# GpSimd's two-operand work on the vector engine, later due times in the SSD tails, and products of ones at the start of a hybrid decoder step

## The chip, the cores and the metric

The kernel runs on one core of one Trainium2 chip. The metric is the device time of one execution in microseconds (us); lower is better. The core's engines are called as the profile calls them: PE (TensorE, the matrix products; PEld are its weight loads), DVE (VectorE), ACT (ScalarE), POOL (GpSimd) and SP (SyncE, which here only issues DMAs). Each engine works through its own instructions in order and waits on semaphores for the others.

## The reference

One decoder layer is computed for a prompt of 512 rows and a sample batch of 8 x 4 rows, D = 1024, all in float32. Cut to its skeleton:

```python
def layer_forward(h, lp, ...):
    u = rmsnorm(h, ffn1_pre_g);  h = h + 0.5 * rmsnorm(swiglu(u, wg, wu, wd), ffn1_post_g)
    u = rmsnorm(h, mix_pre_g)
    z, xbc, dt, q, k, v, qi, ki, wi, g_ssd, g_att = split(u @ w_in)
    y_ssd = ssd_branch(z, xbc, dt, ...)        # causal conv, SSD scan in chunks of 128, norm per group
    y_att = sparse attention on the top 256 keys of an indexer
    merged = sigmoid(g_ssd) * (y_ssd @ w_br_ssd) + sigmoid(g_att) * (y_att @ w_br_att)
    h = h + rmsnorm(merged @ w_out, mix_post_g)
    u = rmsnorm(h, mem_pre_g);   h = h + rmsnorm(mem_attend(u, ...) @ w_mo, mem_post_g)
    u = rmsnorm(h, ffn2_pre_g);  h = h + 0.5 * rmsnorm(swiglu(u, ...), ffn2_post_g)

# ssd_branch, per group of 4 heads:
y = y_diag + y_off + d_skip * xs               # y_diag: (C B^T * decay) @ (x * dt)
y = y * silu(z); y = y * rsqrt(mean(y * y over the group's 256 channels) + EPS) * norm_g
```

## The kernel before, in words

**Layout.** Activations are held transposed: 128 channels on the partitions, 544 columns (512 prompt rows and 32 sample rows) in the free direction, in 8 tiles of a channel block each (`k` = 0..7). `hT` is the residual stream, `y` the output of a stage before its norm. Where 256 or 288 columns are worked on at a time, they are the two halves of the 544.

**Products in two parts.** A float32 factor is split into a high part of reduced precision and the rest (`uh`, `ul` for the activations, `wh`, `wl` for the weights), and `mm` (L291) sums three products per channel block: high x high, low x high, high x low (L310). `weights` (L251) loads 512 KB halves on SP, rounds them on ACT (L270, `wh`) and subtracts on DVE (L271, `wl`); the gates' weights are subtracted on POOL instead (`gates`, L1124).

**Order.** Stages are Python generators that emit instructions and yield `(c, d)`: `c` is the PE time that they have just emitted, `d` a delay before they want to go on, both in a planner's microseconds. `weave` (L104) runs the first generator in its list that is due, and so sets the order in which instructions are emitted. The framework then puts each engine's instructions into a fixed order, which follows the emission with exceptions where it takes an operand to be late.

**Start.** `load_x` (L444) loads the first gain, transposes it on PE (L455) and loads x. `first_T` (L459) transposes the first 256 rows of x (L473), with ACT and DVE writing `uh` and `ul`. Then the FFN's products begin.

**Boundaries between stages.** `bound` (L372) applies the post-norm (L385), adds into `hT` (L386, even `k` on DVE, odd `k` on POOL), squares on ACT and sums the squares into `sqh` on POOL, the last on DVE (`sq_acc`, L363: L366, L369, L370), and writes the next stage's `uh`, `ul` (L391, L392). `rms_rows` (L411) sums the squares over channels by a product with ones (`sth`, L419) and takes the root on DVE; `spread` (L430) copies the factor to all partitions (`pgr`, L439).

**SSD.** `ssd` (L1241) weaves three generators: first the indexer's rounds and the sampled attention, second the tails, last the fronts. A front (`ssd_x`, L1295, and `ssd_z`, L1282) makes the convolved x, B, C of a group (tile `XO`, L1326 to L1329) and z; it may run two groups ahead of the tails. A tail (`ssd_y`, L1338) computes C B^T (`pcb`, L1351) and masks it into `cb` (L1353), transposes B (`pbt`, L1357, copied to `Bt`), after a delay of 2.5 transposes x (`pxt`, L1367; `xd`, `xe` on DVE, L1368 and L1370), multiplies the decay `abc` by `cb` (L1380: POOL, except the second half of groups 1 to 4 on DVE), builds the states (`pst`, L1413), handles the sample rows (with DMAs of `Es` on SP and of the new states), multiplies and adds y, and calls `rms` (L333). That sums squares over the group (`st`, L341), takes the root on DVE (L326 to L331), waits a delay of 4.0, and spreads the factor (L352, `psr`, L355); L1522 applies it and y is stored to `yssd_d`. There are 8 groups.

**Merge.** `att_in`, `att_out` (L1723) and then `merge` (L1738) follow. `merge` reads `yssd_d` back into `yt`, splits it (`yh`, `yl`), and for each of 8 tiles `m` multiplies by the gate (L1760, DVE), adds the attention's part (L1761, POOL) and splits the sum, on which `w_out` works next (`project`, L1767).

Of the kernel before, what the change touches and what calls it, by code (L numbers as in the profile page):

```python
# [7 lines left out]
F32 = mybir.dt.float32  # L8
# [5 lines left out]
ALU = mybir.AluOpType  # L14
# [3 lines left out]
P = 128  # L18
T = 544
TP = 512  # L20
# [148 lines left out]
class Net:  # L169
# [42 lines left out]
    def params(self):  # L212
# [29 lines left out]
        nc.scalar.dma_start(self.caus, I["caus"])  # L242
        ex.close()

    def ps1(self, name="ps1"):
        return self.pm.tile([P, 512], F32, tag="pm", name=name)

# [82 lines left out]
            nc.vector.tensor_tensor(t, t, xh, op=ALU.mult)  # L330
            nc.vector.scalar_tensor_tensor(y, t, 1.5, y, op0=ALU.add, op1=ALU.mult)  # L331

    def rms(self, sqs, inv_n, pool):  # L333


        nc = self.nc
        st = self.ps1("st")
        blk = [(i * P, min(P, T - i * P)) for i in range(5)]
        for i, (c0, n) in enumerate(blk):
            for j, sq in enumerate(sqs):  # L340
                nc.tensor.matmul(st[:n, i:i + 1], sq[:, c0:c0 + n], self.ones[:, :1], start=(j == 0), stop=(j == len(sqs) - 1))  # L341
        w = pool.tile([P, 4, 5], F32, tag="nw", name="nw", bufs=2)
        x, xh, y, t = (w[:, i, :] for i in range(4))
        nc.vector.memset(x, 1.0)
        nc.vector.tensor_scalar(x[:, :4], st[:, :4], inv_n, EPS, op0=ALU.mult, op1=ALU.add)
        nc.vector.tensor_scalar(x[:32, 4:], st[:32, 4:5], inv_n, EPS, op0=ALU.mult, op1=ALU.add)
        self.rsqrt(y, x, xh, t)
        yield 0.3, 4.0

        sq = sqs[0]  # L350
        ps = self.ps1("psr")
        nc.vector.tensor_tensor(sq[:, :TP].rearrange("p (i c) -> p i c", i=4), self.ident.unsqueeze(1).broadcast_to([P, 4, P]),  # L352
                                y[:, :4].unsqueeze(2).broadcast_to([P, 4, P]), op=ALU.mult)
        nc.vector.tensor_scalar(sq[:32, TP:], self.ident[:32, :32], y[:32, 4:], None, op0=ALU.mult)
        nc.tensor.matmul(ps, self.ones, sq[:, :TP], start=True, stop=True)  # L355
        nc.tensor.matmul(st[:, 64:96], self.ones[:32, :], sq[:32, TP:], start=True, stop=True)
        yield 1.0
        return ps, st[:, 64:96]
# [13 lines left out]
    def bound(self, half, sq, post_g, pre_g, rt=None):  # L372


        nc, hT, y = self.nc, self.hT, self.y
        r0, n = HALF[half]
        sl = slice(r0, r0 + n)
        if post_g is not None:
            yield 0.0, 3.0
            r = yield from self.rms_h(sq, half)  # L380
        if pre_g is not None:
            acc = self.nw.tile([P, 288], F32, tag="sqh", name="sqh", bufs=2)
        for k in range(8):
            if post_g is not None:
                nc.vector.scalar_tensor_tensor(y[:, k, sl], y[:, k, sl], post_g[:, k:k + 1], r, op0=ALU.mult, op1=ALU.mult)  # L385
                (nc.gpsimd if k % 2 else nc.vector).tensor_tensor(hT[:, k, sl], hT[:, k, sl], y[:, k, sl], op=ALU.add)  # L386
            if pre_g is not None:
                self.sq_acc(acc, hT[:, k, sl], n, k == 0, last=(k == 7))
            if rt is not None:
                g = pre_g[:, k:k + 1]  # L390
                nc.scalar.activation(self.uh[:, k, sl], hT[:, k, sl], AF.Copy, scale=g)  # L391
                nc.vector.scalar_tensor_tensor(self.ul[:, k, sl], hT[:, k, sl], g, self.uh[:, k, sl].bitcast(F32), op0=ALU.mult, op1=ALU.subtract)  # L392
            yield 0.0, 1.0
        if pre_g is None:
            return
        yield 0.0, 4.0 if rt is None else 8.0
        r = yield from self.rms_h(acc, half)
        if rt is not None:
            nc.scalar.copy(rt[:, sl], r)
            return  # L400
        for k in range(8):
            u = self.nw.tile([P, 288], F32, tag="u", name="u", bufs=2)
            nc.vector.scalar_tensor_tensor(u[:, :n], hT[:, k, sl], pre_g[:, k:k + 1], r, op0=ALU.mult, op1=ALU.mult)
            self.split(self.uh[:, k, sl], self.ul[:, k, sl], u[:, :n], nc.gpsimd if k % 4 == 3 else None)
            yield 0.0, 0.9
# [38 lines left out]
    def load_x(self):  # L444


        nc, I = self.nc, self.I
        xs = self.y.rearrange("p k t -> p (k t)")[:, :4 * D].rearrange("p (i k d) -> i p k d", i=4, k=8)
        self.xin = [xs[i] for i in range(4)] + [self.hT[:32, :, HA:HA + P]]
        gr = self.nw.tile([8, P], F32, tag="dg", name="gr", bufs=2)  # L450
        nc.scalar.dma_start(gr, I["ffn1_pre_g"][0].rearrange("(k p) -> k p", p=P))
        for i in range(2):
            nc.sync.dma_start(self.xin[i], I["x_prompt"][0, i * P:(i + 1) * P, :].rearrange("p (k d) -> p k d", k=8))
        ps = self.ps1("ps_g")
        nc.tensor.transpose(ps[:, :8], gr, self.ident[:8, :8])  # L455
        self.g1 = self.cp.tile([P, 8], F32, name="g1")
        nc.vector.tensor_copy(self.g1, ps[:, :8])

    def first_T(self):  # L459


        nc, I = self.nc, self.I
        q = self.row_squares(0, (0,))
        pss = []
        for k in range(8):
            if k == 4:
                self.weights(("ffn1", "g", 0), [I["ffn1_wg"][0][:, :256]], 8)
            if k % 2 == 0:
                ps = self.ps1("pgx")
                pss.append(ps)  # L470
            v = ps[:, k % 2 * 256:(k % 2 + 1) * 256]
            for i in range(2):
                nc.tensor.transpose(v[:, i * P:(i + 1) * P], self.xin[i][:, k, :], self.ident)  # L473
            gk = self.g1[:, k:k + 1]
            nc.scalar.activation(self.uh[:, k, :HA], v, AF.Copy, scale=gk)
            nc.vector.scalar_tensor_tensor(self.ul[:, k, :HA], v, gk, self.uh[:, k, :HA].bitcast(F32), op0=ALU.mult, op1=ALU.subtract)
        self.weights(("ffn1", "u", 0), [I["ffn1_wu"][0][:, :256]], 8)
        for i in range(2, 4):
            nc.sync.dma_start(self.xin[i], I["x_prompt"][0, i * P:(i + 1) * P, :].rearrange("p (k d) -> p k d", k=8))
        nc.sync.dma_start(self.xin[4], I["x_sample"].rearrange("b t (k d) -> (b t) k d", k=8))  # L480
        for c, ps in enumerate(pss):
            (nc.vector.tensor_copy if c % 2 else nc.scalar.copy)(self.hT[:, 2 * c:2 * c + 2, :HA], ps.rearrange("p (k t) -> p k t", k=2))

        def rest():
            self.row_squares(0, (1,), q)
            yield from self.row_factor(q, 0)

        return rest()
# [849 lines left out]
    def ssd_y(self, g, z):  # L1338
        nc, I, O, sp = self.nc, self.I, self.O, self.sp
# [3 lines left out]
        abc = []  # L1343
# [5 lines left out]
        ps = self.ps1("pcb")  # L1349
        for c in range(4):  # L1350
            nc.tensor.matmul(ps[:, c * P:(c + 1) * P], BO[:, c * P:(c + 1) * P], CO[:, c * P:(c + 1) * P], start=True, stop=True)  # L1351
        cb = sp.tile([P, 4, P], F32, tag="cb", name="cb")
        nc.vector.tensor_tensor(cb, ps.rearrange("p (c t) -> p c t", c=4), self.tri.unsqueeze(1).broadcast_to([P, 4, P]), op=ALU.mult)  # L1353
        yield 0.9
        ps = self.ps1("pbt")
# [1 line left out]
            nc.tensor.transpose(ps[:, c * P:(c + 1) * P], BO[:, c * P:(c + 1) * P], self.ident)  # L1357
        Bt = sp.tile([P, 4, P], F32, tag="hT_", name="Bt", bufs=2)
        nc.scalar.copy(Bt.rearrange("p a b -> p (a b)"), ps)
        yield 0.5, 2.5  # L1360
        hcol = lambda t: t.rearrange("p (c h) -> p c h", c=4)[:, :, 4 * g:4 * g + 4]
        xd = sp.tile([P, 4, 4, 64], F32, tag="xd", name="xd")
        xe = sp.tile([P, 4, 4, 64], F32, tag="xe", name="xe")
        for i in range(2):
            ps = self.ps1("pxt")
# [7 lines left out]
        for i in range(2):  # L1373
            for h in range(2):
                for c in range(4):
                    col = c * 32 + 4 * g + 2 * i + h
                    nc.scalar.activation(abc[i][:, h, c * P:(c + 1) * P], abc[i][:, h, c * P:(c + 1) * P], AF.Relu, scale=-1.0,
                                         bias=self.acs[:, col:col + 1])
            nc.scalar.activation(abc[i], abc[i], AF.Exp, scale=-1.0)
            (nc.vector if 1 <= g <= 4 and i else nc.gpsimd).tensor_tensor(abc[i], abc[i], cb.rearrange("p c t -> p (c t)").unsqueeze(1).broadcast_to([P, 2, TP]), op=ALU.mult)  # L1380

        ps = self.ps1("pcs")
        for q in range(3):
# [27 lines left out]
        for c in range(4):  # L1411
            ps = self.ps1("pst")
# [52 lines left out]
        for i in range(2):  # L1465
# [3 lines left out]
            for q in range(2):  # L1469
                ps = self.ps1("pns")  # L1470
# [8 lines left out]
        ps = self.ps1("pfin")  # L1479
# [10 lines left out]
        for i in range(2):  # L1490
# [7 lines left out]
            ps = self.ps1("pY")  # L1498
# [16 lines left out]
        nc.vector.tensor_tensor(zts[0], zts[0], zts[1], op=ALU.add)  # L1515
        sqs = zts[:1]
        yield 0.0, 9.0
        r, rs = yield from self.rms(sqs, 1.0 / 256, sp)
        for i in range(2):
            tl = 2 * g + i  # L1520
            for o, m in ((Y[i][:, :TP], r), (Y[i][:, TP:], rs)):
# [216 lines left out]
    def merge(self, h_d, rest):  # L1738
# [17 lines left out]
        for m in range(8):  # L1756
            w = self.weights(("w_br_ssd", m), [I["w_br_ssd"][0][:, m * P:(m + 1) * P]], 16)
            t = self.gate(0, m, ep)
            ps = result(self.mm(w, ys, 0))
            nc.vector.tensor_tensor(t, ps, t, op=ALU.mult)  # L1760
            nc.gpsimd.tensor_tensor(t, t, y[:, m, :], op=ALU.add)  # L1761
            self.split(self.uh[:, m, :], self.ul[:, m, :], t)
        ex.close()
        self.open_h()
# [320 lines left out]
```

## Time and profile before

| | us |
|---|---|
| median of 3 runs | 2201.06 (2200.52 to 2204.1) |
| the profiled execution | 2201.23 |
| its span, from the first to the last instruction | 2199.4 |
| PE busy in it | 2101.4 (96%) |
| DVE, ACT, POOL busy | 1324.2 (60%), 955.2 (43%), 444.4 (20%) |
| mean granted clock of PE | 0.979 |

A row of a timeline has the start and the duration in us, the engine, the line of the kernel, the operation, out<-in by tile names, the shapes and the count, and in brackets the idle time of the engine before it and what ended it. A row of waits has the total, the number and the longest. A row of windows gives a stretch, its length, the busy time (and number of instructions) of each engine, the mean granted clock of PE, and DMA share and rate. A row of a line or tile gives the durations in ns (least, median, most) and the first and last start in us. PE overlaps its products, so a busy PE isn't PE at its peak, and a product's duration is longer than the distance to the next one.

### The profile page before, as it was taken

The page shows a single profiled execution, that of the slowest core. Times are in us where ns is not written, and L with a number is a line of the kernel's source. Part 1 is how long each engine was busy: PE and PEld are TensorE (multiplying, and loading weights), DVE is VectorE, ACT ScalarE, POOL GpSimd, SP SyncE. Part 2 cuts the span into 40 slices and gives each one's busy share as a digit, 9 for nine tenths or more (in the row PEclk, how much of TensorE's full clock was granted, in tenths as well). Part 3 has the DMA queues.
Part 4 walks back from the last instruction along what each step waited for, and adds up shares of the span by engine and source line. Part 5 has one row for each costly group of instructions (what it writes and reads, how often), then busy time and mean ns, then how long its engine had stood idle before and what let it go on. Part 6 is the DMA issues. An engine that isn't in the chain of part 4 may idle for free.

```text
span 2199.4 us, 41232 instructions
## 1 busy us (share of the span) xinstructions
PE 2101.4 (96%) x16675; PEld 1960.6 (89%) x16675; DVE 1324.2 (60%) x2711; ACT 955.2 (43%) x1821; POOL 444.4 (20%) x461
## 2 busy tenths in 40 slices
PE   7999999999999999998999999999999979999998
PEld 7999999998788678897888889999987879999998
DVE  6543334475697989896677668544563475424455
ACT  6323345345445665453556445323535443222233
POOL 0000011032122302225555641012320320000011
PEclk9999999999999999998999999999999999999999
DMA  6424565347442223355456636564443433233243
GB/s 199 126 82 128 165 203 197 113 133 213 135 127 83 88 77 110 117 157 161 126 174 192 178 106 186 175 190 155 144 149 139 154 115 115 76 96 90 81 131 100
DMA packets 320107, 301.70 MB, mean 137 GB/s; under 512 B 25416, under 2 KB 290632, under 8 KB 318868
## 3 DMA queue, kind: packets, MB, share of 16 engines
q1 hardware_dynamic: 310508, 272.58, 40.5%
q0 software_dynamic: 8448, 25.18, 3.7%
q8 instruction: 131, 2.15, 0.4%
q10 hardware_dynamic: 960, 1.31, 0.2%
q14 instruction: 60, 0.49, 0.1%
HBM read 261.14 MB, written 37.35 MB: 136 GB/s over the span
## 4 chain that ended last, share of the span: by engine, by line
PE 72%; DVE 13%; DMA 6%; ACT 4%; issue 3%; POOL 2%; SPq 0%; DVEq 0%; ACTq 0%; POOLq 0%
PE pg L310 42%; PE pgh L310 14%; PE pmo L591 2%; DVE wl L271 2%; ACT wh L270 2%; DMA wr<-in_ffn_wu 1%; DVE gtm L1077 1%; DVE XO L1326 1%; DMA yt<-yssd_d 1%; DMA abc<-ac_d 1%; PE pmkT L1811 1%; POOL sqh L370 1%; PE pmo L1878 1%; DVE XO L1329 1%; DMA wr<-in_ffn_wg 1%
## 5 line engine op out<-in xcount | busy, mean ns | idle before, releaser
L270 ACT CAST wh<-wr 128x1024 fp32r<-128x1024 f32 (+3 forms) x362 | 341.6, 959 | 512.1 <-PE pg L310 288.2
L271 DVE TENSOR_TENSOR wl<-wr,wh 128x1024 fp32r<-128x1024 f32 (+3 forms) x338 | 391.1, 1171 | 222.6 <-ACT wh L270 215.8
L310 PE MATMUL pg<-uh,wh 128*128 128x256 f32 (+1 forms) x2336 | 504.1, 297 | 0.8 <-DVE zt L1291 0.8
L310 PE MATMUL pg<-ul,wh 128*128 128x256 f32 (+1 forms) x2336 | 493.4, 292 | 0.0
L310 PE MATMUL pg<-uh,wl 128*128 128x256 f32 (+1 forms) x2336 | 491.6, 291 | 0.0
L310 PEld LDWEIGHTS pg<-uh,wh 128*128 128x128 f32 x2336 | 380.4, 191 | 21.2 <-issue 17.2
L310 PEld LDWEIGHTS pg<-ul,wh 128*128 128x128 f32 x2336 | 381.2, 191 | 2.9 <-issue 2.2
L310 PEld LDWEIGHTS pg<-uh,wl 128*128 128x128 f32 x2336 | 380.0, 190 | 1.8 <-issue 1.4
L310 PE MATMUL pgh<-uh,wh 128*128 128x288 f32 (+2 forms) x880 | 260.8, 299 | 9.5 <-ACT wh L270 6.1
L310 PE MATMUL pgh<-uh,wl 128*128 128x256 f32 (+2 forms) x880 | 260.3, 298 | 7.3 <-DVE wl L271 7.3
L310 PE MATMUL pgh<-ul,wh 128*128 128x256 f32 (+1 forms) x880 | 257.1, 294 | 0.0
L310 PEld LDWEIGHTS pgh<-uh,wh 128*128 128x128 f32 (+1 forms) x880 | 170.4, 195 | 13.2 <-ACT wh L270 7.0
L310 PEld LDWEIGHTS pgh<-uh,wl 128*128 128x128 f32 (+1 forms) x880 | 169.5, 193 | 11.1 <-DVE wl L271 10.1
L310 PEld LDWEIGHTS pgh<-ul,wh 128*128 128x128 f32 x880 | 171.4, 195 | 0.9 <-issue 0.8
L370 POOL TENSOR_TENSOR sqf<-sqf,sqt 128x256 f32<-128x256 f32 (+1 forms) x48 | 52.4, 1092 | 508.9 <-ACT sqt L369 508.6
L310 PE MATMUL pgh<-hh,wh 128*128 128x288 f32 (+1 forms) x352 | 101.9, 290 | 0.0
L310 PE MATMUL pgh<-hh,wl 128*128 128x288 f32 (+1 forms) x352 | 101.2, 288 | 0.3 <-DVE wl L271 0.3
L310 PE MATMUL pgh<-hl,wh 128*128 128x288 f32 (+1 forms) x352 | 101.4, 288 | 0.0
L1326 DVE SCALAR_TENSOR_TENSOR XO<-CB,convw,XO 128x600 f32<-128x600 f32 x96 | 86.2, 899 | 7.1 <-ACT XO L1324 6.6
L702 POOL DMA_INDIRECT G<-in_cache_kidx,ix x16 | 16.4, 1025 | 361.7 <-DVE ix L697 281.2
L617 DVE TENSOR_TENSOR g<-pg,rt 128x544 f32<-128x544 f32 x32 | 23.2, 725 | 101.1 <-PE pg L310 101.1
L620 DVE TENSOR_TENSOR g<-pg,g 128x544 f32<-128x544 f32 x32 | 23.2, 725 | 99.1 <-PE pg L310 99.1
(608 smaller groups left out, 3875.4 us busy)
## 6 DMA issues: line engine op xcount, KB each, us to landing
wr<-in_w_in SPq DMA_DIRECT2D x66, 512.0 KB
wr<-in_ffn_wg SPq DMA_DIRECT2D x48, 512.0 KB
wr<-in_ffn_wu SPq DMA_DIRECT2D x48, 512.0 KB
wr<-in_ffn_wd SPq DMA_DIRECT2D x44, 384.0 KB
wr<-in_ffn_wd SPq DMA_DIRECT2D x44, 320.0 KB
kt_d<-KT SPq DMA_DIRECT2D x8, 1024.0 KB
KT<-kt_d SPq DMA_DIRECT2D x16, 512.0 KB
wr<-in_w_in SPq DMA_DIRECT2D x32, 256.0 KB
```

The lines of the kernel that those rows point to most:

```text
L270: nc.scalar.copy(hi[:, s], r)
L271: (lo_eng or nc.vector).tensor_tensor(lo[:, s], r, hi[:, s].bitcast(F32), op=ALU.subtract)
L310: nc.tensor.matmul(o, a[:, k, c0:c0 + m], x[:, r0:r0 + n], start=(k == 0 and j == 0), stop=(k == KT - 1 and j == 2))
L370: (nc.vector if last else nc.gpsimd).tensor_tensor(acc[:, :n], acc[:, :n], s[:, :n], op=ALU.add)
L591: nc.tensor.matmul(ps[:, :256], a[:, k, i * P:(i + 1) * P], b[:, k, :], start=(k == 0 and j == 0), stop=(k == 7 and j == 2))
L617: nc.vector.tensor_tensor(g1[:, :n], pg, rt[:, sl], op=ALU.mult)
L620: nc.vector.tensor_tensor(g1[:, :n], pu, g1[:, :n], op=ALU.mult)
L1077: nc.vector.scalar_tensor_tensor(G, S, thr[:, j:j + 1], one, op0=ALU.is_ge, op1=ALU.mult, accum_out=cnt[:, j:j + 1])
L1326: nc.vector.scalar_tensor_tensor(xo, CB[:, j:j + 600], cw(j), xo, op0=ALU.mult, op1=ALU.add)
L1329: nc.vector.scalar_tensor_tensor(xo, th, 1.0, xo, op0=ALU.add, op1=ALU.mult)
L1811: nc.tensor.transpose(ps[:, (z * 2 + i) * P:(z * 2 + i + 1) * P], mk[:, i, (k + z) * P:(k + z + 1) * P], self.ident)
L1878: nc.tensor.matmul(ps[:, d * 256:(d + 1) * 256], mv[:, x, h * 256 + d * P:h * 256 + (d + 1) * P], PT[:, x, :], start=(x == 0), stop=(x == 1))
```

## The change

Three kinds of edit. First, three places where POOL added or multiplied two tensors use DVE instead: L386 for odd `k`, L1380 in all groups and halves, L1761. The other two-operand work of POOL (L370, L271 for the gates' weights, a quarter of the splits at L404) stays. Second, two delays of a tail are longer in the groups 0 to 5: 6.0 instead of 2.5 between `Bt` and x's transposes, and 7.0 instead of 4.0 between the root and its spread. Third, 25 products of `ones` (128x128) into a PSUM tile that nobody reads: 4 before the first transpose, 9 after it, and 2, 2 and 8 after the transposes of the channel blocks 1, 3 and 5.

```diff
+    def idle(self, ps, n):
+        for _ in range(n):
+            self.nc.tensor.matmul(ps[:, :P], self.ones, self.ones, start=True, stop=True)
...
-    def rms(self, sqs, inv_n, pool):
+    def rms(self, sqs, inv_n, pool, late=4.0):
...
-        yield 0.3, 4.0
+        yield 0.3, late
...
@@ bound @@
-                (nc.gpsimd if k % 2 else nc.vector).tensor_tensor(hT[:, k, sl], hT[:, k, sl], y[:, k, sl], op=ALU.add)
+                nc.vector.tensor_tensor(hT[:, k, sl], hT[:, k, sl], y[:, k, sl], op=ALU.add)
...
@@ load_x @@
+        self.spare = self.pg.tile([P, 1024], F32, tag="pg", name="spare")
+        self.idle(self.spare, 4)
         ps = self.ps1("ps_g")
         nc.tensor.transpose(ps[:, :8], gr, self.ident[:8, :8])
+        self.idle(self.spare, 9)
...
@@ first_T @@
+            if k in (1, 3, 5):
+                self.idle(self.spare, 2 if k < 5 else 8)
...
@@ ssd_y @@
-        yield 0.5, 2.5
+        yield 0.5, 6.0 if g < 6 else 2.5
...
-            (nc.vector if 1 <= g <= 4 and i else nc.gpsimd).tensor_tensor(abc[i], abc[i], cb.rearrange(...)..., op=ALU.mult)
+            nc.vector.tensor_tensor(abc[i], abc[i], cb.rearrange(...)..., op=ALU.mult)
...
-        r, rs = yield from self.rms(sqs, 1.0 / 256, sp)
+        r, rs = yield from self.rms(sqs, 1.0 / 256, sp, 7.0 if g < 6 else 4.0)
...
@@ merge @@
-            nc.gpsimd.tensor_tensor(t, t, y[:, m, :], op=ALU.add)
+            nc.vector.tensor_tensor(t, t, y[:, m, :], op=ALU.add)
```

More of the change, by code (lines that the diff above doesn't have):

```diff
@@ L1379, in ssd_y @@
             nc.scalar.activation(abc[i], abc[i], AF.Exp, scale=-1.0)
-            (nc.vector if 1 <= g <= 4 and i else nc.gpsimd).tensor_tensor(abc[i], abc[i], cb.rearrange("p c t -> p (c t)").unsqueeze(1).broadcast_to([P, 2, TP]), op=ALU.mult)
+            nc.vector.tensor_tensor(abc[i], abc[i], cb.rearrange("p c t -> p (c t)").unsqueeze(1).broadcast_to([P, 2, TP]), op=ALU.mult)
         ps = self.ps1("pcs")
```

## The prediction

> **What bounds the kernel now.** I read the page first, then who TensorE (PE) waited for, then the granted clock around those waits.
>
> ```profile
> span 2199.4 us, 41232 instructions
> PE 2101.4 (96%) x16675; PEld 1960.6 (89%) x16675; DVE 1324.2 (60%) x2711; ACT 955.2 (43%) x1821; POOL 444.4 (20%) x461
> ```
>
> PE is the bound: the span holds 2199.4 - 2101.4 = 98 us without a product on PE, and only those, and the products run at a lower clock, can be won. This execution took 2201.23 us, 1.8 us more than its span; the median of the runs is 2201.06, so I count from 2201.
>
> ```profile
> PE pxt L1367 <- DVE XO L1329: 10.4, 3, 5.3
> PE sth L419 <- DVE sqh L370: 9.6, 3, 3.8
> PE psr L355 <- DVE zt L352: 7.0, 3, 3.7
> PE pgr L439 <- DVE dg L438: 1.3, 1, 1.3
> 919.00:930.00 11.00, 7.26 (x29) 5.47 (x30) 8.94 (x19) 2.92 (x5) 0.31 (x1) 0.69 0.26 95
> 989.00:999.00 10.00, 4.66 (x26) 3.98 (x25) 9.99 (x18) 1.50 (x3) 1.51 (x2) 0.66 0.21 63
> 1055.00:1063.00 8.00, 5.27 (x23) 4.15 (x23) 6.73 (x20) 4.37 (x7) 0.35 (x2) 0.79 0.28 78
> 1214.00:1224.00 10.00, 5.97 (x38) 4.80 (x37) 8.66 (x12) 0.91 (x2) 8.60 (x7) 0.83 0.25 82
> 1611.00:1620.00 9.00, 5.19 (x29) 4.93 (x29) 6.20 (x22) 2.43 (x6) 2.54 (x3) 0.81 0.50 176
> 1760.00:1774.00 14.00, 8.00 (x43) 7.09 (x42) 9.05 (x24) 7.38 (x14) 2.89 (x4) 0.76 0.45 132
> ```
>
> The first rows are PE's waits (total us, times, longest), the others stretches with each engine's busy time (PE, PE's loads, DVE, ACT, POOL) and then the granted clock. Three waits of 27 us in all are the ones that the change reaches, and a wait has a second price: the clock falls to half. A mean of 0.66 over 10 us is (1-0.66)x10/0.5 = 6.8 us at half.
>
> **Where those waits come from.** In the sixth group of the SSD stage:
>
> ```profile
> 1213.43 5.26 DVE L1329 SCALAR_TENSOR_TENSOR XO<-th,XO 128x600 f32<-128x600 f32 x1
> 1213.38 4.66 POOL L1380 TENSOR_TENSOR abc<-abc,cb 128x1024 f32<-128x1024 f32 x2
> 1218.75 0.65 PE L1367 MATMUL pxt<-ident,XO 128*128 128x128 f32 x4 [4.03 <-DVE XO L1329]
> L1329 DVE SCALAR_TENSOR_TENSOR XO<-th,XO x32: 752/784/5261, 841.4 to 1346.2; 128x600 f32<-128x600 f32 x32
> L1380 POOL TENSOR_TENSOR abc<-abc,cb x12: 2337/2391/3294, 858.5 to 1350.2; 128x1024 f32<-128x1024 f32 x12
> L1380 DVE TENSOR_TENSOR abc<-abc,cb x4: 1216/1220/3226, 933.3 to 1149.8; 128x1024 f32<-128x1024 f32 x4
> L1353 DVE TENSOR_TENSOR cb<-pcb,tri x8: 679/684/692, 857.7 to 1347.1; 128x512 f32<-128x512 f32 x8
> 987.94 2.95 DVE L1326 SCALAR_TENSOR_TENSOR XO<-CB,convw,XO 128x600 f32<-128x600 f32 x1
> 991.14 0.83 DVE L1326 SCALAR_TENSOR_TENSOR XO<-CB,convw,XO 128x600 f32<-128x600 f32 x1
> 987.83 2.42 POOL L1380 TENSOR_TENSOR abc<-abc,cb 128x1024 f32<-128x1024 f32 x1
> 912.72 2.39 DVE L331 SCALAR_TENSOR_TENSOR nw<-nw 128x5 f32<-128x5 f32 x1
> 912.09 5.35 POOL L271 TENSOR_TENSOR wl<-wr,wh 128x1024 fp32r<-128x1024 f32 x2 [3.77 <-ACT wh L270]
> ```
>
> A 0.78 us DVE instruction takes 5.26 and ends 0.6 us after POOL's two products: DVE stands still while POOL holds what both need. The Trainium skill, "SBUF — State Buffer", section "Who interferes with whom", says the same: DVE with two SBUF inputs and a GpSimd instruction that reads SBUF exclude each other for the whole instruction.
>
> **The change part by part.**
>
> *L1380 to DVE (12 products).* Added on DVE 12 x 1.22 = 14.6 us. Removed: stalls. Here 5.26-0.78 = 4.5, at 987.94 2.95-0.83 = 2.1; bounds for the rest: none, or one POOL product each, 10 x 2.4. I take about 14, as much as is added, because DVE is busy in nearly all of these stretches (9.99 of 10, 8.66 of 10). So DVE's load is unchanged, and its late instructions are early. The wait of 4.03 goes by this alone.
>
> *x's transposes due 6.0 instead of 2.5 after Bt, six groups.* The eight groups lie (1347.1-857.7)/7 = 70 us apart, so all pxt waits up to 1218.75 lie in the first six. Each transpose gets 3.5 planner us more. The longest wait, 5.3, is met by 3.5 plus the 2.1 that DVE no longer loses at 987.94; the last of the three is 10.4-5.3-4.0 = 1.1. Taken: 10.4 to 0; bounds 4.0 and 10.4. Next late: xd and xe on DVE, on which the states pst wait; their own delay of 2.5 is kept, so they move with it. So do the rest of the group's steps: four Es loads and five stores on SP, which the next front's weight and state loads now pass, and the memset and copy of CZ on POOL. Nobody waited for these in the rows above, so 0.
>
> *The norm factor's spread due 7.0 instead of 4.0.* 3.0 more against 3.7, 2.7 and 0.5 (the rest of 7.0): 0.7 stays. That one comes from POOL's weight split at L271 (0.16 us of DVE took 2.39), which is kept. Taken 6.3; bounds 0 and 7.0. Behind it go the four L1522 and on SP the group's two stores of yssd, read only in the next stage; but the group ends later (rivals).
>
> *Clock after those waits.* Half clock in the four stretches 919 to 1224: 6.8, 6.8, 3.4 and 3.4 us, 20.4 in all. At most 3.7 + 5.3 of that PE stood anyway, so products ran at half for 11.4 to 20.4 us and lost half of it, 5.7 to 10.2. I take the low end less a tenth for the first stretch, where 0.7 us of wait stays: 5.1. Bounds 0 and 10.2.
>
> *L386 to DVE (28 adds of the boundary's odd tiles) and L1761 (8 adds of merge).*
>
> ```profile
> L386 DVE TENSOR_TENSOR hT<-hT,y x28: 409/453/1065, 461.9 to 2165.0; 128x256 f32<-128x256 f32 x16, 128x288 f32<-128x288 f32 x12
> L386 POOL TENSOR_TENSOR hT<-hT,y x28: 741/920/1662, 462.1 to 2165.1; 128x256 f32<-128x256 f32 x16, 128x288 f32<-128x288 f32 x12
> 1801.90 1.78 POOL L370 TENSOR_TENSOR sqh<-sqh,sqt 128x288 f32<-128x288 f32 x1
> L370 POOL TENSOR_TENSOR sqh<-sqh,sqt x36: 727/808/1779, 463.8 to 1801.9; 128x256 f32<-128x256 f32 x18, 128x288 f32<-128x288 f32 x18
> L1761 POOL TENSOR_TENSOR gt<-gt,y x8: 2387/2401/2413, 1443.9 to 1522.1; 128x544 f32<-128x544 f32 x8
> 1511.23 2.38 DVE L271 TENSOR_TENSOR wl<-wr,wh 128x1024 fp32r<-128x1024 f32 x1
> L319 DVE TENSOR_TENSOR yl<-yt,yh x16: 717/726/727, 1416.5 to 1441.3; 128x544 fp32r<-128x544 f32 x16
> 1525.19 0.51 PE L310 MATMUL pgh<-uh,wh 128*128 128x256 f32 x2 [1.54 <-ACT uh L318]
> ```
>
> The waits sth end a chain that alternates DVE, POOL, ACT, POOL. Four POOL adds per boundary at 0.92 become 0.45, and they no longer queue behind sqh: 4 x 0.47 = 1.9 us less chain against waits of 3.2 on average. I take half of 9.6 = 4.8, and 1.7 of clock (half of the 3.4 us at half clock in 1611 to 1620). Bounds: 0 (the sqh adds stay on POOL and set the pace), and all of 9.6 plus 1.7 plus 3.4 of clock. Added on DVE: 28 x 0.45 = 12.6 us, less stalls of at most 1.07-0.45 each; about +8 on an engine with 40% idle.
>
> L1761: 8 x 0.73 added (the nearest add of that shape), 8 x (2.38-1.22) = 9.3 of stalled L271 removed. Seven lie beside PE's products. The last ends in front of w_out: 2.40-0.73 = 1.67 shorter, so the 1.54 before the first product goes. Taken 1.5; bounds 0 and 1.54.
>
> *Products of ones (25 in the first waits).*
>
> ```profile
> 15.14 0.42 PE L310 MATMUL pgh<-ul,wh 128*128 128x256 f32 x1
> 15.35 0.41 PE L310 MATMUL pgh<-uh,wh 128*128 128x256 f32 x1
> 14.80:18.40 3.60, 3.44 (x13) 3.00 (x14) 1.00 1.01 330
> 18.50:22.10 3.60, 3.60 (x33) 3.60 (x32) 1.00 0.98 279
> ```
>
> The first products start 0.21 apart; in the last row, of L310's products alone like the one above it, 33 fill 3.60 us, 0.11 each: the first run at half clock (the record of the clock begins only after them, its 1.00 there is empty). 13 products at half lose 13 x 0.10 = 1.3 us, and the gaps between them, 3.60 - 13 x 0.21 = 0.9, are transposes at half: 1.8 in all. Downstream stands pgr's 1.3 us wait, which an earlier PE lengthens: bounds -0.5 (a product of ones in front of a transpose) and 1.8. I take 0.8. Their PSUM tile is written by PE alone and read by none; the pool's second buffer serves the first wide product, so 0. The Trainium skill, "TensorE: Matmul & The Clock Gate", Part 1, lets the clock fall again after an idle window of about 3.4 us; should the ones end too early, this term is 0 by it.
>
> *Returns.* Every engine's order is drawn anew.
>
> ```profile
> 830.00:1400.00 570.00, 542.10 (x4529) 489.24 (x4529) 444.24 (x949) 277.50 (x578) 223.84 (x266) 0.97 0.51 151
> ```
>
> Of 570 us PE is busy for all but 27.9; pxt and psr are 17.4 of that, 10.5 lie elsewhere. I take nearly as much again as new waits, +9 (bounds 0 and 20, the whole of the two), and +1 for DVE's load.
>
> Sum: -10.4 -6.3 -5.1 -4.8 -1.7 -1.5 -0.8 +9 +1 = -20.6 us from 2201.2, so **2181**, 0.9% less.
>
> **Rivals.** (1) The waits move on: the gains of the SSD stage (21.8) are given back by the next late instruction, since POOL's L271 and L370 still stop DVE. Left: 30.6 - 21.8 - 1 = 8, so 2193. For it speaks the row at 912.72, against it that the longest stalls are L1380's. (2) The lock works the other way: more two-input adds on DVE hold up POOL's sqh (1.78 at 1801.90 against 0.81), and the sth waits stay: 4.8 + 1.7 less, 2187. The skill's section named above says that issue order decides who blocks; the row agrees. (3) The due times do nothing, because the scheduler places instructions by readiness, and DVE's added 32 us eat the stalls: 2199, no change. (4) Slower: the groups' tails become the chain.
>
> ```profile
> 1342.00 1.13 PE L355 MATMUL psr<-zt,ones 128*128 128x512 f32 x2
> 1342.97 0.38 PE L1351 MATMUL pcb<-XO,XO 128*128 128x128 f32 x2
> L1748 SPq DMA_DIRECT2D yt<-yssd_d x16: 319/320/417, 1411.7 to 1437.0; - x16
> ```
>
> A tail's first products (pcb) follow the last tail's spread at once. Six tails 3.5 + 3.0 later are 39 us at most; the yt loads behind them already last until 1437. If a third (13 us) reaches the end, and the SSD gains with it fall to 0, it is 2201 - 8 + 13 = 2206. It decides from about 8 us of delay on. Against it: fronts and sampled attention fill PE in the first six groups.
>
> **Chances.** The forecast 0.54, (1) 0.15, (2) 0.11, (3) 0.08, (4) 0.12. Faster by over 0.2% (4.4 us, about what can be told from no change) 0.80, within 0.08, slower 0.12. Low end: all terms full and no returns is -46 or 2155, which I hold unlikely; 2166. High end 2198, which takes in (1) and (2); the likeliest case alone 2168 to 2190.
>
> **What would show it.** POOL has no L1380, L386, L1761; L1329's longest is under 2.5 us; pxt and psr leave the top of PE's waits, and half-clock stretches between 900 and 1230 get fewer; the wait before w_out goes; the first products start 0.12 apart. I am wrong if pcb's last group starts later than 1345, or if new waits of over 15 us stand in the SSD stage.

## The result, and the profile after

The changed kernel takes 2168.5 us (median of 4 runs, 2167.0 to 2170.1) against 2200.9 us of the kernel before (2200.5 to 2204.1) beside it: a ratio of 0.985 (95% interval 0.9833 to 0.9867), 32 us faster. The forecast was 2181 with a range of 2166 to 2198.

The profiled execution of the changed kernel, the first lines of its page, then PE's waits, then three lines of instructions, two of DVE and one of POOL (least, median, most in ns). Lines of the kernel moved by 5 up to `ssd_y` and by 10 from there: L1329 is now L1339, L1380 is L1390, L355 is L360, L419 is L424.

```profile
span 2165.3 us, 41287 instructions
PE 2096.3 (97%) x16725; PEld 1963.0 (91%) x16725; DVE 1324.1 (61%) x2759; ACT 956.2 (44%) x1821; POOL 377.7 (17%) x413
```

```profile
PE sth L424 <- DVE sqh L375: 8.6, 4, 3.6
PE psr L360 <- DVE zt L357: 6.0, 3, 3.3
...
PE pg L315 <- ACT yh L323: 3.8, 3, 2.4
```

```profile
L1339 DVE SCALAR_TENSOR_TENSOR XO<-th,XO x32: 753/780/785, 844.0 to 1314.7; 128x600 f32<-128x600 f32 x32
L1390 DVE TENSOR_TENSOR abc<-abc,cb x16: 1217/1222/1226, 861.7 to 1330.8; 128x1024 f32<-128x1024 f32 x16
L375 POOL TENSOR_TENSOR sqh<-sqh,sqt x36: 733/888/1711, 463.8 to 1765.0; 128x256 f32<-128x256 f32 x18, 128x288 f32<-128x288 f32 x18
```

The 5.26 us instruction of L1329 is gone (longest 785 ns), pxt is no longer among the waits, DVE's busy time is the same 1324 us although it does 48 instructions more. But psr and sth, which the change was also to reach, still stand at the top.

Where the time went is read from four stretches, cut at products of PE: up to the last indexer product (pcl) +3.4 us; the SSD stage from there to the merge's first product, with the attention behind the SSD, -33.3; the merge, up to the first product of w_out, +5.9; from there to the end -10.2. Columns: stretch, length, busy time of PE, PEld, DVE, ACT, POOL, granted clock, DMA. The SSD stage, the merge, and 300 us from the first copy of w_out's results on, before:

```profile
824.18:1421.80 597.62, 569.72 (x4750) 514.32 (x4751) 457.02 (x968) 286.13 (x593) 223.84 (x266) 0.97 0.51 151
1421.80:1521.00 99.20, 97.53 (x770) 96.04 (x769) 45.87 (x44) 28.00 (x36) 16.81 (x7) 1.00 0.53 166
1527.20:1827.20 300.00, 277.62 (x2124) 252.77 (x2123) 163.18 (x389) 138.73 (x287) 66.30 (x73) 0.97 0.43 142
```

The same three after:

```profile
827.62:1391.94 564.32, 552.83 (x4750) 504.79 (x4750) 453.78 (x979) 287.45 (x592) 198.52 (x254) 0.99 0.54 161
1391.94:1497.05 105.11, 101.17 (x769) 98.97 (x769) 42.36 (x52) 27.35 (x37) 2.02 (x1) 0.97 0.49 153
1501.10:1801.10 300.00, 284.59 (x2185) 260.20 (x2185) 174.37 (x414) 143.77 (x293) 52.23 (x57) 0.97 0.45 148
```

In the SSD stage PE's idle time (length less busy) fell from 27.9 to 11.5 us, and its busy time by 16.9 us for the same 4750 products. The record of the clock has 37.5 us at half in this stage before and 7.1 after; half of the difference is 15.2. In the 300 us behind the merge the idle time fell from 22.4 to 15.4 us. The stages of one profile are not exact, though: the kernel with spare memsets below, whose order on PE, DVE, ACT and SP is the changed kernel's, reaches pcl 7.0 us earlier and takes 11.7 us longer for the SSD stage, and its ratio is nearly the same.

### The profile page after: what moved, and what is told of

It is laid out like the page before. It is cut to its first block, busy times and chain, and to the rows that moved or that the text cites. A ratio compares the mean times of both kernels' runs of the same rounds, so it can differ in the third digit from the quotient of the medians.

```text
span 2165.3 us, 41287 instructions
## 1 busy us (share of the span) xinstructions
PE 2096.3 (97%) x16725; PEld 1963.0 (91%) x16725; DVE 1324.1 (61%) x2759; ACT 956.2 (44%) x1821; POOL 377.7 (17%) x413
## 4 chain that ended last, share of the span: by engine, by line
PE 77%; DVE 12%; DMA 4%; ACT 4%; issue 2%; POOL 0%; SPq 0%; DVEq 0%; ACTq 0%; POOLq 0%
PE pg L315 44%; PE pgh L315 17%; PE pmo L601 2%; DVE wl L276 2%; DVE gtm L1087 1%; ACT wh L275 1%; DMA abc<-ac_d 1%; DMA yt<-yssd_d 1%; DMA wr<-in_ffn_wg 1%; DMA wr<-in_ffn_wu 1%; PE ph L1448 1%; PE pmkT L1821 1%; PE pqk L1199 1%; PE pmo L1888 1%; PE pms L1877 1%
## 5 line engine op out<-in xcount | busy, mean ns | idle before, releaser
L276 DVE TENSOR_TENSOR wl<-wr,wh 128x1024 fp32r<-128x1024 f32 (+3 forms) x338 | 377.3, 1128 | 210.6 <-ACT wh L275 206.2
L1336 DVE SCALAR_TENSOR_TENSOR XO<-CB,convw,XO 128x600 f32<-128x600 f32 x96 | 82.8, 863 | 13.7 <-ACT XO L1334 13.1
```

The lines of the kernel that those rows point to most:

```text
L276: (lo_eng or nc.vector).tensor_tensor(lo[:, s], r, hi[:, s].bitcast(F32), op=ALU.subtract)
L1336: nc.vector.scalar_tensor_tensor(xo, CB[:, j:j + 600], cw(j), xo, op0=ALU.mult, op1=ALU.add)
```

## The experiments

Theory A: POOL's work on two SBUF operands stops DVE, and a stopped DVE stops PE; that is most of the gain. Theory B: the later due times carry most of it. The runs were made in three groups, in which the kernel before took 2200.6, 2210.1 and 2215.2 us; kernels of different groups are therefore compared by their ratio to it. The changed kernel was not timed again in groups 2 and 3. Ratios, with 95% intervals:

| kernel | group | us | ratio to before |
|---|---|---|---|
| changed | | 2168.5 | 0.985 (0.9833 to 0.9867) |
| three POOL moves only | 1 | 2175.1 | 0.9888 (0.9869 to 0.9907) |
| due times only | 1 | 2182.9 | 0.9916 (0.9901 to 0.9931) |
| products of ones only | 1 | 2198.5 | 0.9998 (0.9985 to 1.0012) |
| abc (L1380) only | 1 | 2185.1 | 0.9928 (0.9912 to 0.9943) |
| abc and due times | 2 | 2199.3 | 0.9951 (0.9933 to 0.997) |
| changed + spare POOL products | 2 | 2189.5 | 0.9907 (0.9892 to 0.9921) |
| changed + spare POOL memsets | 2 | 2178.0 | 0.9862 (0.9846 to 0.9878) |
| changed, due times in groups 0 to 3 | 2 | 2189.1 | 0.9907 (0.989 to 0.9925) |
| changed, L386's odd k on POOL again | 3 | 2193.3 | 0.9908 (0.9894 to 0.9922) |
| changed, without the late spread | 3 | 2205.8 | 0.9955 (0.994 to 0.9969) |
| changed, gates' wl on DVE | 3 | 2166.8 | 0.979 (0.9776 to 0.9804) |
| the same, sums of squares on DVE too | 3 | 2159.3 | 0.975 (0.9737 to 0.9764) |

**Each part alone.** The three POOL moves:

```diff
-(nc.gpsimd if k % 2 else nc.vector).tensor_tensor(hT...)                # L386
+nc.vector.tensor_tensor(hT...)
-(nc.vector if 1 <= g <= 4 and i else nc.gpsimd).tensor_tensor(abc...)   # L1380
+nc.vector.tensor_tensor(abc...)
-nc.gpsimd.tensor_tensor(t, t, y...)                                     # L1761
+nc.vector.tensor_tensor(t, t, y...)
```

> Of the change only the three places of GpSimd work given to DVE (L386, L1380, L1761). Theory A (GpSimd's two-operand work stops DVE, and that stops PE): this part carries most of the 32 us, so 2176 to 2184 us; L1329 has no instruction over 2.5 us. Theory B (the due times give DVE's late results the time they need, whoever made them late; the moved work only changes sides): 2191 to 2196 us, from the boundaries and merge alone.

The middle one of these alone:

> Of the change only L1380 (12 products of 128x1024 on DVE). Theory A: the SSD stage gets most of its gain, 2182 to 2190 us. Theory B: DVE's load is as before, 2196 to 2201 us.

The due times alone (`yield 0.5, 6.0 if g < 6 else 2.5` and 7.0 for 4.0 in `rms`):

> Of the change only the two later due times (6.0 and 7.0 in groups 0 to 5). Theory A: the stalls of 4.5 and 2.1 us stay on DVE, so little is won, 2192 to 2201 us, and with the tails 6.5 us later it may be slower. Theory B: the waits pxt and psr go, 2176 to 2186 us.

And the 25 products of ones alone:

> Of the change only the 25 products of ones. Both theories: within 2199.5 to 2201.5 us. By the prediction -0.8 us; by the changed kernel's trace, where the first product starts at 15.0 and the clock is half from 16.1 to 19.5, nothing. If it is under 2198 us, something later depends on the start and both are wrong on this part.

The SSD stage of the three moves; then that of abc alone, with two of its waits; then that of the due times alone, with one:

```profile
821.20:1403.89 582.69, 567.80 (x4751) 512.83 (x4751) 452.02 (x981) 287.87 (x594) 197.16 (x254) 0.98 0.51 156
```

```profile
824.69:1404.45 579.76, 565.89 (x4751) 510.21 (x4751) 450.94 (x980) 287.28 (x592) 198.89 (x254) 0.98 0.52 155
```

```profile
PE psr L355 <- DVE zt L352: 5.3, 4, 3.7
...
PE pxt L1367 <- DVE XO L1329: 0.6, 1, 0.6
```

```profile
821.64:1395.94 574.30, 555.17 (x4751) 506.89 (x4751) 453.15 (x967) 287.85 (x592) 225.87 (x266) 0.99 0.53 158
```

```profile
PE psr L355 <- DVE zt L352: 6.8, 3, 3.6
```

abc alone does what theory A said: 15.5 us, pxt from 10.4 to 0.6, PE's idle time in the stage from 27.9 to 13.9. The other two moves add 10 us, outside the stage (582.7 us with them, 579.8 without). But the due times alone give 17.8 us, where A expected 0 to 9 and B 15 to 25: each theory is right about its own part. With the due times alone pxt is gone too, the SSD stage is shorter still, and psr stands at 6.8, nearly as before; the merge then takes 107.5 us, 8 us longer than before, and with abc alone 99.6. So each part is worth more than half of the whole, and 25.5 + 17.8 = 43 against 32: a wait such as pxt, which both remove, can be won once only. The ones alone give 2198.5, 1 us below the range expected, and change nothing that can be told (0.9985 to 1.0012).

**Is it POOL's reading that stops DVE, or only that abc came late?** To the changed kernel, where DVE makes abc, POOL gets work that nobody needs at the 12 old places: three products of two operands, or, as a control of about the same length, one copy of 8 columns and six memsets. The order of the instructions on PE, DVE, ACT and SP is that of the changed kernel in both, row for row.

```diff
+[nc.gpsimd.tensor_tensor(spare, cb[:, :3], cb[:, 1:], op=ALU.mult) for j in range(3)]   # one kernel
+nc.gpsimd.tensor_copy(spare[:, 0, :8], cb[:, 0, :8])                                     # the other
+[nc.gpsimd.memset(spare, 0.0) for j in range(6)]
```

> The changed kernel, with extra work on POOL that nobody needs: at each of the 12 places where POOL multiplied abc before, three products of two operands (128x384, cb by cb, into a spare tile). The order of instructions on PE, DVE, ACT and SP is the one of the changed kernel, row for row; abc itself is still made on DVE. Theory A (what hurt before was that DVE stands still while POOL works on two SBUF operands, and PE then waits): DVE's stalls beside these products add up to 10 us or more, single DVE instructions take over 2 us again, and the time goes up by 5 to 16 us: 2173 to 2185. Rival (what hurt was that abc came late from the slower POOL, and the stop of DVE costs little because DVE has slack): within 2 us of the changed kernel, 2166 to 2171.

> As the kernel with the spare products, but POOL's extra work is one copy of 8 columns of cb and six memsets of 128x384 at each of the 12 places, about as long, and reading nothing from SBUF but the 8 columns. The order on the other four engines is again that of the changed kernel. Theory A (the stop comes from POOL's reading of two operands): no stalls of DVE beside the memsets, and the time of the changed kernel, 2166 to 2171. Rival (any long work of POOL at these places costs time, because the copies and gathers that queue behind it on POOL come late): as slow as the kernel with the products, 2173 or more.

With products, then with memsets (the line's instructions, then the SSD stage):

```profile
L1390 POOL TENSOR_TENSOR spr<-cb x36: 992/1016/3374, 857.1 to 1356.7; 128x384 f32<-128x384 f32 x36
L1390 DVE TENSOR_TENSOR abc<-abc,cb x16: 1212/1224/2048, 857.7 to 1353.7; 128x1024 f32<-128x1024 f32 x16
```

```profile
823.60:1414.91 591.31, 564.08 (x4750) 508.94 (x4751) 463.65 (x979) 287.97 (x592) 241.62 (x290) 0.99 0.51 153
```

```profile
L1390 POOL MEMSET spr<- x72: 408/418/523, 857.5 to 1338.6; 128x384 f32 x72
L1390 DVE TENSOR_TENSOR abc<-abc,cb x16: 1214/1218/1226, 855.5 to 1336.1; 128x1024 f32<-128x1024 f32 x16
```

```profile
820.61:1396.65 576.04, 559.22 (x4750) 508.42 (x4750) 453.12 (x979) 287.84 (x592) 230.02 (x338) 0.99 0.53 157
```

Same order, same chip, extra work that takes about as long where nothing disturbs it (36 products of 1.0 us, 37 us of copies and memsets), and 11.5 us between them (2189.5 and 2178.0). Their ratios times 2200.9 are 2180.4 and 2170.5, in the range of theory A both times. Beside the products DVE's instructions lose about 10 us in some 20 places (time over the lower quartile of the same line and shape), beside the memsets 0.7 us in 3, and with the products DVE's busy time in the stage is 10.5 us longer. It works both ways: a spare product of 1.0 us once took 3.4, beside five instructions of DVE. The products held POOL for 46 us in all, 9 more than the memsets, so a share of the 11.5 us may come from POOL's own work behind them, but most of PE's new waits in the stage are for results of DVE. So a product on POOL that reads SBUF costs PE time although nobody waits for its result; memsets cost nothing that can be told (0.9862 against 0.985, and the intervals overlap). The Trainium skill, "SBUF — State Buffer", section "Who interferes with whom", says that a DVE instruction with two SBUF inputs contends with a GpSimd instruction that reads SBUF and not with one that only writes it; this pair shows both halves.

**Do the parts add up?** abc and the due times together:

> Only the abc products (L1380) on DVE and the two due times; the adds of L386 and L1761 stay on POOL and there are no products of ones. L1380 alone gave 2185 us, the due times alone 2183, the whole change 2168.5, the three DVE moves together 2175. Theory A (the parts shorten different waits, L386 and L1761 are worth what they were beside L1380 alone, 2185 - 2175 = 10, mostly in the boundaries' sth waits after 1500 us): 2173 to 2180, with the gain of the SSD stage complete, the merge starting within 5 us of where it does in the whole change, and about 8 us lost after that. Rival (L1380 and the due times remove the same stalls, so that the second adds little): 2180 to 2186.

Neither theory: 2199.3 us, a gain of 0.5% where abc alone had 0.7% and the due times alone 0.8%. In the SSD stage the order of every engine is that of the changed kernel, and yet it takes 589.9 us, in the same group of runs in which the kernel with memsets took 576.0:

```profile
826.13:1416.02 589.89, 565.16 (x4750) 513.49 (x4751) 452.98 (x979) 287.74 (x592) 193.77 (x254) 0.98 0.52 154
```

```profile
1080.59 1.02 PE L1413 MATMUL pst<-xe,Bt 128*128 128x256 f32 x4
...
1086.41 0.37 ACT L1416 COPY H<-pst 128x256 f32<-128x256 f32 x1 [10.77 <-remote]
...
1086.84 2.07 PE L1413 MATMUL pst<-xe,Bt 128*128 128x256 f32 x4 [5.11 <-ACT H L1416]
```

One place of it: by the trace the products `pst` have ended at 1081.61; ACT's copy of the first, which waits for PE's semaphore alone, starts 4.8 us later, and PE stands for 5.1 us. ACT is not late. In the trace's record of semaphore updates, which the rows don't show, PE raises its semaphore for its last four products together, from 1086.35 to 1086.46, and the copy starts 0.06 us after the first raise. The ends of products are modelled in a trace, so either these products ran later than it has them, or their raises were held back. At the same place of the changed kernel each raise comes 0.02 us after its product's end, and the copy follows 0.63 us after the first product's start:

```profile
1074.71 1.03 PE L1423 MATMUL pst<-xe,Bt 128*128 128x256 f32 x4
...
1075.34 0.37 ACT L1426 COPY H<-pst 128x256 f32<-128x256 f32 x1 [6.34 <-PE pst L1423]
```

Four of the kernels below show the same stop there, of 4.6 to 5.0 us and with the same late raises, and the one without the late spread has one of 3.8 us; no other trace has it at this place. What is behind it is not in the trace, and it stays open. The stop is part of what these kernels lose against the changed kernel, and no run shows whether their edits bring it.

**Edits undone one at a time.** The due times in groups 0 to 3 only (`g < 4`):

> The changed kernel with the later due times (6.0 and 7.0) in groups 0 to 3 only; groups 4 to 7 have the old 2.5 and 4.0. Theory A (the 12.7 us that the changed kernel gives back between the last product of att_out and the first of the merge come from tails that end later relative to att_out, so that yssd is read back late): the gap from att_out's last product to merge's first shrinks from 32.8 towards 20 us, and the time to 2160 to 2166. Rival (in groups 4 and 5 the later due times earn as much as they give back): 2166 to 2173. A second rival (they earned the waits of these groups, which come back): above 2173.

The mechanism of the first theory is there, its gain is not. The gap that it names is one of DVE's instructions, from its last multiplication by a gate in att_out (L1745) to its first in the merge (L1770), while PE makes the merge's first tile; it shrinks from 32.8 to 21.1 us, and the merge takes 100.6 us instead of 105.1. But the ratio is 0.9907, 12 us above the changed kernel, as the second rival had it. PE's idle time in the SSD stage is 29.4 us:

```profile
821.48:1419.03 597.55, 568.19 (x4751) 512.62 (x4751) 452.25 (x979) 286.99 (x592) 193.28 (x254) 0.97 0.51 151
```

```profile
PE psr L360 <- DVE zt L357: 7.8, 5, 3.3
PE pst L1423 <- ACT H L1426: 5.0, 1, 5.0
PE pst L1423 <- issue: 3.7, 1, 3.7
```

The waits that this rival means don't come back, though: pxt is not there, and psr grows by 1.8 us only. The two pst rows are the stop and a second one like it at 1220.8, with PE's raise 3.6 us late, so 8.7 us of the idle time are of unknown cause, and what the due times earn in groups 4 and 5 stays open.

The spread of the norm factor due 4.0 again, x's transposes still 6.0:

> The changed kernel without the later spread of the norm factor (4.0 planner us in all groups); x's transposes keep 6.0. Theory A (the prediction's term: the later spread is worth 6.3 us of psr waits and some clock): psr waits back at 7 us or more, ratio 0.988 to 0.991. Rival (in the changed kernel psr still waits 6.0 of the 7.0 us, so the later spread earns nothing there): 0.983 to 0.987.

Theory A has the wait right and its price too low, and the rival is wrong: 0.9955, two thirds of the gain gone. The SSD stage takes 610.2 us, more than the 597.6 in the profile of before, and 44 us of it are at half clock:

```profile
819.60:1429.75 610.15, 577.45 (x4750) 518.15 (x4751) 449.20 (x979) 286.82 (x592) 193.18 (x254) 0.96 0.49 149
```

```profile
PE psr L360 <- DVE zt L357: 11.7, 5, 4.2
```

With x's transposes put off and the spread not, psr is worse than it ever was (11.7 us, against 7.0 before): in this kernel the two delays belong together.

L386's odd k on POOL again:

> The changed kernel with one edit undone: the boundary's adds for odd k (L386 of before) are on POOL again. Theory A (these adds shorten the boundaries' chain and nothing else): the waits sth between 1500 and 1800 us go back from about 7 to 9 us or more, the SSD stage takes what it takes in the changed kernel, and the ratio to before is 0.987 to 0.990, some 5 to 10 us above the changed kernel's 0.985. Rival (the kernel with the due times and the abc products alone came out at 0.995 because small edits outside the SSD stage shift its timing): 0.991 to 0.996, with the loss inside the SSD stage. If the adds are worth nothing: 0.984 to 0.986.

```profile
1517.10:1817.10 300.00, 279.05 (x2112) 254.76 (x2111) 163.09 (x389) 138.48 (x286) 67.77 (x73) 0.94 0.43 144
```

```profile
PE sth L424 <- DVE sqh L375: 9.5, 3, 3.8
...
PE pst L1423 <- ACT H L1426: 4.7, 1, 4.7
```

0.9908, 13 us above the changed kernel: part of it is theory A's (idle time after w_out 21.0 us instead of 15.4, at a clock of 0.94 instead of 0.97), part is in the SSD stage, which this edit does not touch (585.5 us, with the stop described above), as the rival had it.

**More of the same.** What POOL still multiplies in the changed kernel held DVE for 22.1 us (wl, mostly the gates') and 23.5 us (sums of squares).

```diff
-w = self.win((C_GS, C_GA)[x] + c * 256, lo_eng=self.nc.gpsimd)
+w = self.win((C_GS, C_GA)[x] + c * 256)
```

> The changed kernel with the gates' weights subtracted on DVE, not POOL (L271 of before): about 1.2 us more on DVE for each, and the POOL products of 2.46 us gone that held DVE for 22.1 us in all in the changed kernel. Theory A (what DVE gains in stalls is worth as much here as it was for abc, where 18.5 us of stalls gave 15 us): 0.978 to 0.983. Rival (DVE pays about as much for the work as it gains, and PE does not wait here): 0.984 to 0.988.

```diff
-(nc.vector if last else nc.gpsimd).tensor_tensor(acc[:, :n], acc[:, :n], s[:, :n], op=ALU.add)
+nc.vector.tensor_tensor(acc[:, :n], acc[:, :n], s[:, :n], op=ALU.add)
```

> As the kernel before it, and the sums of squares (L370 of before, 84 adds) on DVE as well: POOL has almost no products of two operands left. Theory A: the chain of a boundary alternates between DVE and ACT alone, the waits sth fall from 8.6 us to 4 to 6, and it gains 2 to 6 us on the kernel with the gates alone. Rival (84 x 0.45 = 38 us more on DVE, of which 23.5 us are stalls that go, at places where DVE works without a break: wl of the weights comes late): 0 to 8 us slower than the kernel with the gates alone.

The first gives 0.979, in theory A's range, and its psr waits are 0.2 us in all, against 6.0 in the changed kernel. The second gives 0.975, 7.5 us less than the first, where theory A had 2 to 6: 1% less time than the changed kernel, with intervals apart, and the fastest here, although both have the stop. The stretch that holds the gates (from the first product pdt to pcl) of the changed kernel, then of the one with both edits, with its page, its wait sth, and its 300 us from the first copy of w_out's results on:

```profile
549.70:827.50 277.80, 265.01 (x1988) 214.67 (x1989) 222.62 (x598) 151.52 (x350) 62.96 (x37) 0.96 0.33 101
```

```profile
545.90:812.70 266.80, 259.27 (x1989) 210.49 (x1989) 221.21 (x610) 151.93 (x350) 33.16 (x25) 0.99 0.34 106
1498.10:1798.10 300.00, 288.42 (x2247) 263.98 (x2246) 180.97 (x469) 146.92 (x298) 3.72 (x9) 0.98 0.46 151
```

```profile
PE 2088.9 (97%) x16725; PEld 1954.7 (91%) x16725; DVE 1324.6 (62%) x2859; ACT 957.8 (44%) x1821; POOL 245.7 (11%) x313
```

```profile
PE sth L424 <- DVE sqh L375: 2.2, 2, 2.0
```

DVE took 100 products more than in the changed kernel and is busy for 1324.6 us, as before all changes: the stalls that went cost as much of its time as the work that came. sth falls from 8.6 to 2.2 us only now, when the whole chain of a boundary is off POOL.

## Why the prediction was right, and where its steps were not

The time is inside the range, 12.5 us below the forecast, at the edge of the likeliest case's own range (2168 to 2190). The mechanism, that POOL's products stop DVE and DVE then PE, is right. The terms are right in part, and the one for the clock misses by 12 us, as much as the forecast itself.

- *L1380 to DVE.* Right in mechanism, and near in size. It was to add as much on DVE as it takes away; with L1380 alone DVE's busy time falls by 6.2 us, so the stalls were worth about 21 us, not 14. The spare products show the stop by itself.
- *x's transposes, pxt 10.4 to 0.* The wait went, but the term was shared out wrongly: 4.0 was given to L1380 and the rest to the due time. abc alone leaves 0.6, the due times alone leave none. Each suffices, so the sum of parts is not the whole.
- *The spread, psr 6.3 less.* Failed: 7.0 became 6.0, and with the due times alone 6.8. One of the two long waits went (2.7 at 1058.2), the other shrank (3.7 to 2.5), and a new one of 3.3 us stands at 988.9, near the place where pxt had waited 5.3. The work before psr was late, not the spread early: a step of the root that takes 0.17 us in the median takes 2.37 beside two of POOL's weight splits for the gates, which the change kept, and DVE then works without a break until it has made psr's operand.

```profile
975.95 4.91 POOL L276 TENSOR_TENSOR wl<-wr,wh 128x1024 fp32r<-128x1024 f32 x2 [0.48 <-ACT wh L275]
978.51 2.37 DVE L331 TENSOR_SCALAR nw<-nw 128x5 int32<-128x5 int32 x1
```

  The prediction had seen such a split at 912.09 and charged it 0.7 us; rival 1 named it as the reason why waits would move on. With these splits on DVE psr waits 0.2 us. Still the delay is needed in the changed kernel, since without it the ratio is 0.9955. Its worth was not in the row from which it was read.
- *Clock after those waits, 5.1.* The worst term: the stage's busy time fell by 16.9 us for the same products. Four stretches with 20.4 us at half were counted, and of those the low end was taken; by the record of the clock the stage had 37.5 us at half before and 7.1 after, behind other waits too.
- *L386, 4.8 + 1.7.* The size is right (PE's idle time in the 300 us after w_out -7.0), the wait is not: sth went from 9.6 to 8.6 only. Its two long waits there halved (3.8 to 1.7 and 3.6 to 1.8 us), and a third of 3.6 us came instead at 1768. Other waits behind a boundary, such as one of 2.5 us for wl, are gone. Rival 2 had expected the sth waits to stay, because sqh's adds stay on POOL; the waits nearly did, and the adds' median went from 808 to 888 ns, but the time was won all the same.
- *L1761, 1.5.* Right: the wait of 1.54 us, which stood 21 products into w_out, is gone.
- *Ones, 0.8.* Wrong: nothing that can be told. The first products do start 0.12 us apart, and fall to 0.21 a microsecond later:

```profile
15.03 0.39 PE L315 MATMUL pgh<-uh,wh 128*128 128x256 f32 x1 [2.74 <-ACT wh L275]
15.26 0.28 PE L315 MATMUL pgh<-ul,wh 128*128 128x256 f32 x1
15.38 0.29 PE L315 MATMUL pgh<-uh,wh 128*128 128x256 f32 x1
...
16.71 0.42 PE L315 MATMUL pgh<-uh,wh 128*128 128x256 f32 x1
16.92 0.41 PE L315 MATMUL pgh<-ul,wh 128*128 128x256 f32 x1
```

  The last product of ones ends 2.74 us ahead of the first real one, and the 3.4 us at half clock come all the same, only later (16.1 to 19.5). That is the case for which the prediction named the clock gate's idle window. It is not certain to come: of the nine kernels with these products, two (without the late spread, and gates' wl on DVE) keep the full clock there, after a wait as long.
- *Returns, +9.* Near in size, and not where it was looked for. In the SSD stage pxt and psr together were to give 16.7 us of idle time, and the stage's idle time did fall by 16.4, although psr gave 1.0 only: other waits, such as one of 3.7 us at 1285.8, went too. What came back is at the merge. PE waits 2.4 us ahead of its first product there for yh, made from a yt that is read late, and then takes 5.9 us longer although the merge's adds left POOL (rows above): its idle time in the merge grows from 1.7 to 3.9 us, and 6.8 us from 1391.7 on are at half clock. This is rival 4's place, at 8.3 of its 13 us. The later due times bring it: the merge takes 104.6 to 107.5 us in the kernels that have both in groups 0 to 5, 97.6 to 99.9 in those that have neither. Rival 4's mark, pcb's last group later than 1345, did not come: it starts at 1320.4.

Rival 3, that the due times do nothing, falls with the due times alone (0.9916). What no step foresaw is how little the parts add: abc 0.7%, due times 0.8%, both 0.5%, all POOL moves and both 1.5%; and each of three edits taken out of the whole costs 0.6 to 1.1%, with the stop in it. Why abc and the due times together earn less than either alone is shown only as far as the stop goes. The forecast treated each wait as a term with a price of its own. That was close enough for the whole, because its range was wide and a term too large (psr) stood against one too small (the clock), and would have been wrong for several of its parts.

## What to carry to other kernels

Where a DVE instruction in the trace takes several times its usual duration and ends with a POOL instruction that reads SBUF, move POOL's instruction to DVE and count the stall against the added work; here the two were nearly equal on DVE, and PE gained 15.5 us from L1380 alone. Two edits that remove the same wait are worth it once, and a wait's row tells who was late, not which delay would cure it: try each part alone and the whole without each part before crediting one. Cut a stage at the same product of PE in both kernels and compare the counts of products, or work that has moved across the cut counts as a gain. The products of ones ended 2.74 us ahead of the first real one and earned nothing; whether ones that reach up to it would was not tried.

## What the runs showed of the hardware that was not expected

- Waits of PE below 3 us can bring half clock: in the changed kernel, after one of 1.72 us at 1585.2 the record shows 3.4 us at half from 1586.2 on, and after one of 2.74 us before the first product 3.4 us. Not each does: after 1.91 us at 287.2 and 2.50 us at 928.8 the clock stayed full. Except for the last one of a trace, the stretches last 3.4 us or two, three or four times that (13.7 at 514.4). The Trainium skill, "TensorE: Matmul & The Clock Gate", Part 1, puts the fall after an idle window of about 3.4 us; the lengths agree with it, the idle times measured here are shorter.
- PE's semaphore can come late: in five traces the raises for four products came within 0.12 us of each other, 4.2 us or more after the last `pst` among them had ended by the trace, and the copy that waited for them started at once. The cause stays open.
- Identical orders on PE, DVE, ACT and SP do not give identical times: in one group of runs the SSD stage took 576.0 us with memsets on POOL, and 589.9 us with nothing more on POOL than the changed kernel has there. The stop of 5.1 us is a third of that difference.
